# Column sums four abreast, float32r gate sums, two products of ones and a moved split in a TensorE-bound hybrid backbone

## The chip, the cores and the metric

The kernel runs on one core of one Trainium2 chip. A core has a matrix engine (TensorE, "PE" in the profile, with its weight loads "PEld"), VectorE ("DVE"), ScalarE ("ACT"), GpSimd ("POOL") and SyncE ("SP"), each with its own instruction queue. Here SP issues nearly all loads from the chip's main memory (HBM) and POOL the stores. TensorE multiplies a stationary tile (loaded as weights, here up to 128x128) with a moving tile of up to 512 columns and writes to PSUM, the accumulator memory; everything else reads and writes SBUF. The metric is the device time of one execution in microseconds (us).

## The reference

Two layers over 512 latent tokens and 256 context tokens, width 1024, all in float32. Layer 0 is bidirectional retention with 4 heads, layer 1 a chunked gMLP with a spatial gate. Around each layer stand a conditioned RMSNorm and a conditioned gate:

```python
silu_c = jax.nn.silu(c)
silu_cc = jax.nn.silu(c_ctx)
for i in range(DEPTH):                                   # DEPTH = 2
    shift_x, scale_x, gate_x = jnp.split(silu_c @ ada_w[i] + ada_b[i], 3, axis=-1)
    shift_c, scale_c, gate_c = jnp.split(silu_cc @ ada_w[i] + ada_b[i], 3, axis=-1)
    hx = rmsnorm(x, norm_g[i]) * (1 + scale_x[:, None]) + shift_x[:, None]
    hc = rmsnorm(ctx, norm_g[i]) * (1 + scale_c) + shift_c
    # i = 0: retention of hx and hc;  i = 1: gMLP of hx
    x = x + gate_x[:, None] * out_x
return rmsnorm(x, final_g)
```

Retention projects to q, k (256 per head), v and z (512 per head), turns q and k of the latent tokens by their grid position, weights the scores by a decay in both directions, normalizes the head's output, multiplies it with silu(z) and projects back to 1024. The gMLP projects to u, v and z of 2048 each, normalizes v, mixes it inside chunks of 128 tokens, and projects u * mixed * silu(z) back to 1024.

The change touches how four vectors of 1024 are made that are not needed at once: `gate_x` of layer 0, and shift, scale and gate of layer 1, each a product of `silu(c)` with a 1024x1024 block of `ada_w`.

## The kernel before

**Precision.** Each float32 operand of a large product is split in two float32r tiles, a high part (an ACT copy that rounds) and a low part (a DVE subtraction, `split`), and a product is three float32r products (`mm3`). In the trace the split tiles are called `hl`, the raw weights `raw`; `oA11` to `oA22` and `oS1` to `oS4` are split activations and their sums, `hc` the split context.

**Projections.** Layer 0's q, k, v and z are computed in twelve "quads" (`QUADS`). A "kq" quad makes k and q of one head with the weights stationary (`features`, shown as moving tile oA, oS or hc, stationary hl: `pst<-oA,hl`); a "vz" quad makes half of v and z of one head with the activations stationary (`tokens`, shown as `pst<-hl,oA`). A quad is a block product by seven products of sums (names B11, T1, T2, B21, T3, B22, T4); each is a group of 24 matmuls of 128x128 by 128x256, and B11 and B21 have a second group of 24 for the context. The first three quads are treated apart; the other nine are the loop over `QUADS[3:]`, numbered n = 0 to 8: vz, vz, kq, vz, vz, kq, vz, kq, vz. The quads n = 2, 5 and 7 are the second, third and fourth kq quad.

**Order.** PE runs in the order of the text. ACT and DVE are ordered by a scheduler at build time. Work that is not urgent is written as generators, and the loop takes single steps of them between products (`aside`, `step`): `background` makes the four vectors; `dec0`, `qk0` and `v0` prepare the decay, q and k, and v of head 0. `load_qk` issues five loads in three steps (k, q, k, the context's k, q), then splits each of the five tiles (`halves`) in a step of its own. `Q` streams the weights through slots w0 to w6 and splits them two products ahead.

**Background.** For each of the four vectors DVE multiplies 8 blocks of 128x1024 by a per-row scalar and adds them up in `a` (`ada_a` in the trace). What is left is a sum over the 128 rows. For the first three vectors `columns` does it: two f32 products with 32 columns of ones, each over 512 columns and each in its own 32 columns of the array; a copy of 64 rows to SBUF (`cole`); four transposes of 64x128 blocks; a DVE copy that picks out one column per block. For the fourth, two f32 products with 128x128 ones give the sum on all rows, and DVE adds a bias (`gateb1`). Three of these events lie among the projection quads, the fourth in the scores of head 2.

**Products of ones.** `between_modes` is one f32 product of a 128x128 tile of ones with itself whose result nobody reads. `inside_t` is a list of functions to be called inside the next `tokens` product, in front of its second of four blocks (behind 6 of its 24 matmuls). Before the change one is put there at n = 0.

After the projections come per head `attend` (scores, products with v, normalization) and `project_out`, then layer 1. Head 0's first scores read q and k as split by `load_qk`. Layer 1's first weights are read into freed slots, w2 and w3 among them, as soon as these come free.

Of the kernel before, what the change touches and what calls it, by code (L numbers as in the profile page):

```python
# [8 lines left out]
F32R = mybir.dt.float32r  # L9
# [4 lines left out]
P = 128  # L14
D = 1024
# [11 lines left out]
HS = 256  # L27
# [6 lines left out]
def f32(ap):  # L34
    return ap.bitcast(F32)
# [32 lines left out]
def hybrid_kernel(ctx, tc, xT_d, cT_d, cv_d, sv_d, rows_d, ada0_d, adag_d, w_d, rope_d, dec_d, ws_d, id_d, out_d):  # L68
    nc = tc.nc
    pe, act, dve, sp = (Queue(tc, e) for e in (nc.tensor, nc.scalar, nc.vector, nc.sync))  # L70
# [11 lines left out]
    def st(shape, tag, dt=F32, bufs=1, name=None):  # L82
        return sb.tile(shape, dt, tag=tag, name=name or tag, bufs=bufs)
# [34 lines left out]
    def t2(name, shape=(P, 512), dt=F32):  # L118
        return st(list(shape), "t2", dt, bufs=T2, name=name)

    def pt(shape=(P, 512), tag="ps"):
        return ps.tile(list(shape), F32, tag=tag, name="pst", bufs=6 if tag == "ps" else 2)

    mm = pe.matmul
# [7 lines left out]
    def split(hl, src, late=None):  # L132
        h, l = hl
        act.copy(h, src)
        low = lambda: dve.tensor_tensor(l, src, f32(h), ALU.subtract)
        if late is None:
            low()
        else:
            late.append(low)
# [4 lines left out]
    def load(dst, src):  # L144
        sp.dma_start(dst, src)
# [282 lines left out]
    ones = st([P, P], "ones")  # L428
# [3 lines left out]
    ident = st([P, P], "ident")  # L432
# [203 lines left out]
    def project(q):  # L636
        if q[0] == "kq":
            return Product(features, kq_done(q[1]), hc)
        return Product(tokens, vz_done(q[1], q[2]), hc)
# [192 lines left out]
    def ada_piece(i, tag, tags):  # L832
        a = st([P, D], tag, name="ada_a")
        rows = []
        for k in range(KT + 1):
            if k < KT:
                rows.append(bg_raw(tags))
                load(rows[k], adag_d[8 * i + k])
            if k == 0:
                yield None  # L840
                continue
            r, c = rows[k - 1], cpad[:, k - 1, 0:1]
            if k == 1:
                dve.tensor_scalar(a, r, c, None, ALU.mult)
            else:
                dve.scalar_tensor_tensor(a, r, c, a, ALU.mult, ALU.add)
            yield None
        yield a

    def columns(a, dst):  # L850
        pr = pt(tag="tm")
        for j in range(2):
            mm(pr[32 * j:32 * j + 32, :], ones[:, 0:32], a[:, j * 512:j * 512 + 512], start=True, stop=True)
        e = t2("cole")
        act.copy(e[0:64, :], pr[0:64, :])
        yield
        pq = pt((P, 4, 64), tag="tm")
        for b in range(4):
            pe.transpose(pq[:, b, :], e[0:64, b * P:b * P + P], ident[0:64, 0:64])
        v = pq.rearrange("p b (j r) -> p r j b", r=32)  # L860
        dve.tensor_copy(dst.rearrange("p (j b) -> p j b", j=2), v[:, 0, :, :])

    gate0 = st([P, KT], "gate0")
    gs1 = st([P, KT], "gs1")
# [3 lines left out]
    def background():  # L868
        for i in range(4):
            a = None  # L870
            for a in ada_piece(i, *(("g1", ("g2", "g3")) if i < 3 else ("oA22", ("w2", "w3")))):
                if a is None:
                    yield
            yield
            if i == 0:
                yield from columns(a, gate0)
                dve.tensor_tensor(gate0, gate0, gateb0, ALU.add)
            elif i == 1:
                yield from columns(a, sh1)
                dve.tensor_tensor(sh1, sh1, adab1[:, 0, :], ALU.add)  # L880
                dve.tensor_tensor(shs, sh1[:, 0:4], sh1[:, 4:8], ALU.add)
            elif i == 2:
                yield from columns(a, gs1)
                dve.tensor_tensor(gs1, gs1, adab1[:, 1, :], ALU.add)
                dve.scalar_tensor_tensor(gs1, gs1, 1.0, g1, ALU.add, ALU.mult)
            else:
                gb = st([P, D], "g1", name="gateb1")
                load(gb, rows_d[0:1, :].partition_broadcast(P))
                yield
                yield  # L890
                yield
                for j in range(2):
                    pr = pt(tag="tm")
                    mm(pr, ones, a[:, j * 512:j * 512 + 512], start=True, stop=True)
                    dve.tensor_tensor(gb[:, j * 512:j * 512 + 512], pr, gb[:, j * 512:j * 512 + 512], ALU.add)
                Q.gate = gb
            yield i

    bg = background()

    def aside(work):

        act.pinned = dve.pinned = True
        r = next(work, None)
        act.pinned = dve.pinned = False
        return r

    def step():
        return aside(bg)
# [83 lines left out]
    def popped():  # L993
        if later:
            later.pop(0)()
# [18 lines left out]
    v0 = load_v(0)  # L1014
    for n, q in enumerate(QUADS[3:]):
        pr = project(q)
        if n == 0:
            inside_t.append(between_modes)
        for i, name in enumerate(SINGLE):
            pr.run(name, Q.get())  # L1020
            if i % 2:
                popped()
            if 2 not in pieces and i not in (2, 4):
                pieces.append(step())
            if n == 5 and i % 2 == 0:
                aside(dec0)
            if n >= 6:
                aside(qk0)
            if n == 8:
                aside(v0)  # L1030
# [586 lines left out]
```

## Time and profile before

| | us |
|---|---|
| median of 3 runs (878.61 to 880.75) | 878.79 |
| profiled execution | 878.75 |
| its span, first to last instruction | 876.7 |
| PE busy in it | 866.0 |
| DVE busy | 712.2 |
| ACT busy | 457.2 |
| POOL busy | 58.3 |

Around the span lie 2.05 us. Rows of the profile name the engine, the operation, `out<-in` by the names of tiles (for a matmul: PSUM tile, moving tile, stationary tile), the shape and a count. In the timeline a row is a run of like instructions, with its start and its duration from the start of the first to the modelled end of the last; starts of neighbouring rows are the sounder measure. An f32 product that isn't a transpose leaves two records, a float32r product and a transpose one. All instructions have line L54, the helper that records them, so work is told apart by tile names.

### The profile page before, as it was taken

The page shows a single profiled execution, that of the slowest core. Times are in us where ns is not written, and L with a number is a line of the kernel's source. Part 1 is how long each engine was busy: PE and PEld are TensorE (multiplying, and loading weights), DVE is VectorE, ACT ScalarE, POOL GpSimd, SP SyncE. Part 2 cuts the span into 40 slices and gives each one's busy share as a digit, 9 for nine tenths or more (in the row PEclk, how much of TensorE's full clock was granted, in tenths as well). Part 3 has the DMA queues.
Part 4 walks back from the last instruction along what each step waited for, and adds up shares of the span by engine and source line. Part 5 has one row for each costly group of instructions (what it writes and reads, how often), then busy time and mean ns, then how long its engine had stood idle before and what let it go on. Part 6 is the DMA issues. An engine that isn't in the chain of part 4 may idle for free.

```text
span 876.7 us, 16965 instructions
## 1 busy us (share of the span) xinstructions
PE 866.0 (99%) x6890; PEld 826.8 (94%) x6890; DVE 712.2 (81%) x997; ACT 457.2 (52%) x707; POOL 58.3 (7%) x96
## 2 busy tenths in 40 slices
PE   8999999999999999999999999999999999999997
PEld 7799999999999999998989999999999899899986
DVE  4689978699789877878677688999899488688995
ACT  4465744444545435736255548844666546256434
POOL 0001211002101101000000001111000000000110
PEclk9999999999999999999999999999999999999999
DMA  9932967457677458848344511645435135035522
GB/s 349 405 129 97 303 239 267 150 174 241 193 237 243 145 165 328 286 127 272 132 156 158 165 52 70 200 153 196 142 133 180 36 121 192 25 121 168 121 44 102
DMA packets 75774, 153.81 MB, mean 175 GB/s; under 512 B 7728, under 2 KB 34864, under 8 KB 75696
## 3 DMA queue, kind: packets, MB, share of 16 engines
q1 hardware_dynamic: 67392, 128.40, 44.2%
q0 software_dynamic: 7872, 24.12, 8.2%
q8 instruction: 54, 0.88, 0.4%
q10 hardware_dynamic: 432, 0.20, 0.1%
q14 instruction: 24, 0.20, 0.1%
HBM read 128.58 MB, written 24.12 MB: 174 GB/s over the span
## 4 chain that ended last, share of the span: by engine, by line
PE 96%; DVE 1%; DMA 1%; ACT 1%; issue 0%; DVEq 0%; ACTq 0%
PE pst L54 96%; DMA raw<-in_w_dram 1%; DMA xq<-in_xT_dram 0%; DVE o L54 0%; ACT junk L54 0%; DVE xq L54 0%; DVE bnx L54 0%; DVE oA L54 0%; ACT oA L54 0%; ACT fss L54 0%; DVE gs L54 0%; DVE hl L54 0%; DVE sq L54 0%; ACT o L54 0%; DVE ada_s L54 0%
## 5 line engine op out<-in xcount | busy, mean ns | idle before, releaser
L54 DVE TENSOR_TENSOR hl<-raw,hl 128x1024 fp32r<-128x1024 f32 (+2 forms) x197 | 234.8, 1198 | 67.8 <-ACT hl L54 67.5
L54 ACT CAST hl<-raw 128x1024 fp32r<-128x1024 f32 (+2 forms) x197 | 202.8, 1033 | 137.1 <-DVE raw L54 59.3
L54 PE MATMUL pst<-oS,hl 128*128 128x256 f32 x1104 | 133.9, 279 | 0.1
L54 PE MATMUL pst<-hl,oS 128*128 128x256 f32 x1152 | 133.4, 276 | 0.0
L54 PEld LDWEIGHTS pst<-hl,oS 128*128 128x128 f32 x1152 | 131.8, 188 | 1.0 <-ACT snap L54 0.8
L54 PEld LDWEIGHTS pst<-oS,hl 128*128 128x128 f32 x1104 | 129.3, 188 | 1.6 <-PE pst L54 0.8
L54 PE MATMUL pst<-oA,hl 128*128 128x256 f32 x936 | 117.2, 280 | 1.7 <-DVE hl L54 1.2
L54 PEld LDWEIGHTS pst<-oA,hl 128*128 128x128 f32 x936 | 111.2, 188 | 4.5 <-DVE hl L54 1.6
L54 DVE TENSOR_TENSOR raw<-raw 128x1024 f32<-128x1024 f32 x92 | 111.9, 1218 | 0.8
L54 ACT COPY snap<-pst 128x512 f32<-128x512 f32 x92 | 53.6, 584 | 90.5 <-PE pst L54 90.3
L54 PE MATMUL pst<-hl,oA 128*128 128x256 f32 x768 | 91.6, 277 | 0.0
L54 PE MATMUL pst<-og,hl 128*128 128x256 f32 x768 | 91.1, 278 | 0.0
L54 PEld LDWEIGHTS pst<-og,hl 128*128 128x128 f32 x768 | 89.2, 188 | 0.3
L54 PEld LDWEIGHTS pst<-hl,oA 128*128 128x128 f32 x768 | 89.2, 188 | 0.1
L54 PE MATMUL pst<-v,ph 128*128 128x512 f32 x192 | 59.8, 393 | 0.0
L54 PE MATMUL pst<-hl,ya 128*128 128x512 f32 (+1 forms) x246 | 59.1, 386 | 0.0
L54 PEld LDWEIGHTS pst<-hl,ya 128*128 128x128 f32 x246 | 45.3, 188 | 9.5
L54 DVE TENSOR_TENSOR snap<-pst,snap 128x512 f32<-128x512 f32 x69 | 47.2, 684 | 6.2 <-PE pst L54 6.2
L54 PE MATMUL pst<-hl,hc 128*128 128x256 f32 x384 | 46.1, 276 | 0.0
L54 PEld LDWEIGHTS pst<-hl,hc 128*128 128x128 f32 x384 | 44.7, 188 | 0.0
L54 ACT CAST ph<-pf 128x512 fp32r<-128x512 f32 x24 | 14.8, 619 | 54.1 <-DVE pf L54 53.6
L54 PEld LDWEIGHTS pst<-v,ph 128*128 128x128 f32 x192 | 36.1, 188 | 7.3 <-issue 0.2
(181 smaller groups left out, 1022.3 us busy)
## 6 DMA issues: line engine op xcount, KB each, us to landing
raw<-in_w_dram SPq DMA_DIRECT2D x224, 256.0 KB, 4.1
bg<-in_adag_dram SPq DMA_DIRECT2D x32, 512.0 KB, 4.4
ada_w<-in_ada_dram SPq DMA_DIRECT2D x16, 512.0 KB, 9.1
raw<-in_w_dram SPq DMA_DIRECT2D x16, 512.0 KB, 4.3
bg<-in_dec_dram SPq DMA_DIRECT2D x12, 512.0 KB, 4.8
v<-snap POOLq DMA_DIRECT2D x16, 256.0 KB, 5.3
z<-snap POOLq DMA_DIRECT2D x16, 256.0 KB, 5.1
v<-v SPq DMA_DIRECT2D x8, 512.0 KB, 3.8
```

Of the source, the lines that this page charges most:

```text
L54: made = op(*args, **kw)
```

## The change

In `columns`, the two f32 products of 512 columns become four of 256, each in its own 32 columns of the array, so that the sum stands on 128 rows of 256; ACT copies 128x256 instead of 64x512; two transposes of 128x128 take the place of four of 64x128. For the fourth vector, `a` is split in a float32r pair in slots w2 and w3 (one ACT copy and one DVE subtraction of 128x1024), the ones are copied to float32r, and four float32r products that accumulate in pairs take the place of two f32 products. A product of ones is also put into the first token product of n = 3 and n = 8. And the steps of `qk0` are taken at the first three products of n = 6 and at all products of n = 8, where they were taken at every product from n = 6 on.

```diff
     def columns(a, dst):
-        pr = pt(tag="tm")
-        for j in range(2):
-            mm(pr[32 * j:32 * j + 32, :], ones[:, 0:32], a[:, j * 512:j * 512 + 512], start=True, stop=True)
-        e = t2("cole")
-        act.copy(e[0:64, :], pr[0:64, :])
+        pr = pt((P, HS), tag="tm")
+        for j in range(4):
+            mm(pr[32 * j:32 * j + 32, :], ones[:, 0:32], a[:, j * HS:j * HS + HS], start=True, stop=True)
+        e = t2("cole", (P, HS))
+        act.copy(e, pr)
         yield
-        pq = pt((P, 4, 64), tag="tm")
-        for b in range(4):
-            pe.transpose(pq[:, b, :], e[0:64, b * P:b * P + P], ident[0:64, 0:64])
+        pq = pt((P, 2, P), tag="tm")
+        for b in range(2):
+            pe.transpose(pq[:, b, :], e[:, b * P:b * P + P], ident)
...
                 load(gb, rows_d[0:1, :].partition_broadcast(P))
+                ones_r = st([P, P], "rs0", F32R, name="ones_r")
+                act.copy(ones_r, ones)
+                hl = [st([P, D], tag, F32R, name="ada_h") for tag in ("w2", "w3")]
                 yield
+                split(hl, a)
                 yield
                 yield
                 for j in range(2):
                     pr = pt(tag="tm")
-                    mm(pr, ones, a[:, j * 512:j * 512 + 512], start=True, stop=True)
+                    for m in range(2):
+                        mm(pr, ones_r, hl[m][:, j * 512:j * 512 + 512], start=m == 0, stop=m == 1, skip_group_check=True)
...
         pr = project(q)
-        if n == 0:
+        if n in (0, 3, 8):
             inside_t.append(between_modes)
...
-            if n >= 6:
+            if n == 8 or (n == 6 and i < 3):
                 aside(qk0)
```

How the instructions stand, at the places that matter. The first is PE in the second kq quad (n = 2), where the first background piece is summed: rows are products in their order, moving tile before stationary tile, with the number of the buffer behind some names.

```order
 L54 MATMUL pst<-oA_291,hl 128x256 x24
 L54 MATMUL pst<-hc,hl 128x256 x24
-L54 MATMUL pst<-ada_a,ones 32x512 x2
+L54 MATMUL pst<-ada_a,ones 32x256 x4
 L54 MATMUL pst<-oS_865,hl 128x256 x24
-L54 MATMUL pst<-ident,cole 128x64 x4
+L54 MATMUL pst<-ident,cole 128x128 x2
 L54 MATMUL pst<-oS_1013,hl 128x256 x24
 L54 MATMUL pst<-oA_574,hl 128x256 x24
```

Sums and transposes keep their places; their shapes and counts change. The second piece stands the same way in a vz quad, the third in the fourth kq quad (n = 7).

The second is PE at the end of that kq quad and the start of the vz quad behind it (n = 3); the same difference stands behind the fourth kq quad (n = 8).

```order
 L54 MATMUL pst<-oS_1177,hl 128x256 x24
 L54 MATMUL pst<-oA_576,hl 128x256 x24
-L54 MATMUL pst<-hl,oA_291 128x256 x24
+L54 MATMUL pst<-hl,oA_291 128x256 x6
+L54 MATMUL pst<-ones 128x128
+L54 MATMUL pst<-hl,oA_291 128x256 x18
 L54 MATMUL pst<-hl,hc 128x256 x24
 L54 MATMUL pst<-hl,oS_865 128x256 x24
```

The product of ones goes behind the sixth matmul of the first token product.

The third is the gate sum. On PE, among the products of head 2's weights with v:

```order
 L54 MATMUL pst<-v,pl 128x512
 L54 MATMUL pst<-v,ph 128x512 x2
-L54 MATMUL pst<-ada_a,ones 128x512 x2
+L54 MATMUL pst<-ada_h,ones_r 128x512 x4
 L54 MATMUL pst<-v,pl 128x512
 L54 MATMUL pst<-v,ph 128x512 x2
```

The place is the same, the products are others. On DVE, at the end of head 1's output projection (accumulator updates, then the first score weights of head 2):

```order
-L54 SCALAR_TENSOR_TENSOR acc<-pst,gate_896,acc 128x256 x8
+L54 SCALAR_TENSOR_TENSOR acc<-pst,gate_896,acc 128x256 x5
+L54 TENSOR_TENSOR ada_h<-ada_a,ada_h 128x1024
+L54 SCALAR_TENSOR_TENSOR acc<-pst,gate_896,acc 128x256 x4
 L54 SCALAR_TENSOR_TENSOR pf<-pst,dt 128x512
 L54 TENSOR_TENSOR pl<-pf,ph 128x512
```

The low part of the split comes between the accumulator updates (the piece of the difference also moved one update from in front of v's splits).

The fourth is ACT in the last quad (n = 8), up to the split of v. Before:

```order
L54 COPY snap<-pst 128x512
L54 CAST hl<-raw 128x1024
L54 COPY snap<-pst 128x512
L54 CAST hl<-raw 128x1024
L54 COPY snap<-pst 128x512
L54 ACTIVATE snap<-snap 128x512
L54 CAST v<-v 128x1024
```

And after:

```order
L54 CAST qk<-qk 128x512
L54 CAST hl<-raw 128x1024
L54 COPY snap<-pst 128x512
L54 CAST qk<-qk 128x512
L54 CAST hl<-raw 128x1024
L54 COPY snap<-pst 128x512
L54 CAST qk<-qk 128x512
L54 CAST hl<-raw 128x1024
L54 COPY snap<-pst 128x512
L54 CAST qk<-qk 128x512
L54 ACTIVATE snap<-snap 128x512
L54 CAST qk<-qk 128x512
```

The five copies of q and k, which stood among the splits of the seventh and eighth quad, stand between those of the last; the subtractions on DVE follow them in the same way.

More of the change, by code (lines that the diff above doesn't have):

```diff
@@ L850, in columns @@
     def columns(a, dst):
-        pr = pt(tag="tm")
-        for j in range(2):
-            mm(pr[32 * j:32 * j + 32, :], ones[:, 0:32], a[:, j * 512:j * 512 + 512], start=True, stop=True)
-        e = t2("cole")
-        act.copy(e[0:64, :], pr[0:64, :])
+        pr = pt((P, HS), tag="tm")
[3 more added lines that the diff above has]
+        act.copy(e, pr)
         yield
-        pq = pt((P, 4, 64), tag="tm")
-        for b in range(4):
-            pe.transpose(pq[:, b, :], e[0:64, b * P:b * P + P], ident[0:64, 0:64])
+        pq = pt((P, 2, P), tag="tm")
+        for b in range(2):
+            pe.transpose(pq[:, b, :], e[:, b * P:b * P + P], ident)
         v = pq.rearrange("p b (j r) -> p r j b", r=32)
-        dve.tensor_copy(dst.rearrange("p (j b) -> p j b", j=2), v[:, 0, :, :])
+        dve.tensor_copy(dst.rearrange("p (j b) -> p j b", j=4), v[:, 0, :, :])
     gate0 = st([P, KT], "gate0")
```

## The prediction

> **What bounds the kernel now.** I read the page first: its times, the busy table and the chain that ended last.
>
> ```profile
> span 876.7 us, 16965 instructions
> PE 866.0 (99%) x6890; PEld 826.8 (94%) x6890; DVE 712.2 (81%) x997; ACT 457.2 (52%) x707; POOL 58.3 (7%) x96
> PE 96%; DVE 1%; DMA 1%; ACT 1%; issue 0%; DVEq 0%; ACTq 0%
> ```
>
> PE is busy for 99% of the span and is 96% of the chain. The view of waits, for PE, starts with its largest entry:
>
> ```profile
> PE pst L54 <- DVE sq L54: 1.4, 2, 1.2
> ```
>
> The largest total that PE waited for anybody is 1.4 us. So this kernel's time is the sum of what PE issues, one instruction behind the other, and an edit counts if it takes something out of that row, puts something in, or changes the pace of what stays. Moving work between ACT and DVE counts only if PE ends up waiting. A busy PE says nothing of its pace, though; that is read from start times in the timeline. Columns there: start, duration of the merged row, operation, count. I use differences of starts, since the ends of pipelined matmuls are modelled.
>
> The change touches four places on PE. The second background piece (a column sum, then transposes) lies in a run of token products:
>
> ```profile
> 222.44 2.88 PE L54 MATMUL pst<-hl,hc 128*128 128x256 f32 x24
> 225.25 1.05 PE L54 MATMUL pst<-ada_a,ones 128*32 128x512 f32 x4
> 226.23 5.73 PE L54 MATMUL pst<-hl,oS 128*128 128x256 f32 x48
> 231.89 0.46 PE L54 MATMUL pst<-ident,cole 64*128 64x64 f32 x4
> 232.28 3.01 PE L54 MATMUL pst<-hl,oA 128*128 128x256 f32 x24
> 235.12 2.99 PE L54 MATMUL pst<-oA,hl 128*128 128x256 f32 x24
> ```
>
> The sums hold PE from 225.25 to 226.23, 0.98 us, and the transposes from 231.89 to 232.28, 0.39 us. (An ordinary f32 product shows as two records, a transpose as one.) A product of ones, as the change adds two, stands here, with an undisturbed group behind it:
>
> ```profile
> 108.70 0.38 PE L54 MATMUL pst<-ones 128*128 128x128 f32 x2
> 108.84 2.30 PE L54 MATMUL pst<-hl,oA 128*128 128x256 f32 x18
> 110.98 2.88 PE L54 MATMUL pst<-hl,hc 128*128 128x256 f32 x24
> 113.70 0.28 PE L54 MATMUL pst<-hl,oS 128*128 128x256 f32 x1
> ```
>
> The undisturbed group takes 113.70 - 110.98 = 2.72 us for 24, 113 ns each: the fast pace. A features product (weights stationary) runs at another one:
>
> ```profile
> 292.37 5.92 PE L54 MATMUL pst<-oS,hl 128*128 128x256 f32 x48
> 298.13 2.99 PE L54 MATMUL pst<-oA,hl 128*128 128x256 f32 x24
> 300.96 2.99 PE L54 MATMUL pst<-hc,hl 128*128 128x256 f32 x24
> 312.26 2.90 PE L54 MATMUL pst<-hl,oA 128*128 128x256 f32 x24
> 315.00 1.18 PE L54 MATMUL pst<-hl,hc 128*128 128x256 f32 x9
> ```
>
> Here 24 take 300.96 - 298.13 = 2.83 us, 118 ns each, although the shape is the same. This pace is not fixed to the kind of product, as the start of the program shows below, so it is a term of its own.
>
> **The change part by part: the column sums.** Three pieces. Two f32 products of 512 columns become four of 256, each in its own 32 columns of the array. The same form stands in the conditioning of layer 0:
>
> ```profile
> 21.45 1.07 PE L54 MATMUL pst<-ada_w,cpad 128*32 128x256 f32 x16
> 22.45 0.97 PE L54 MATMUL pst<-oA,hl 128*128 128x256 f32 x6
> ...
> 24.89 0.84 PE L54 MATMUL pst<-oS,hl 128*128 128x256 f32 x6
> 25.66 1.93 PE L54 MATMUL pst<-ada_w,cpad 128*32 128x256 f32 x32
> 27.52 1.68 PE L54 MATMUL pst<-oA,hl 128*128 128x256 f32 x12
> ```
>
> Sixteen records (8 products) take 22.45 - 21.45 = 1.00 us and 32 take 27.52 - 25.66 = 1.86, so 16 more cost 0.86 and 8 more 0.43. The change's 8 records then take 1.00 - 0.43 = 0.57 us in place of 0.98. Gain 0.41 each, 1.23 for three. Ends: 0 (the four do not run abreast) and 0.98 - 0.43 = 0.55 each (no fixed part); I take 0.41, since it comes from the same form. The Trainium skill, page "TensorEngine Tiling (Array Packing)", section Theoretical Speedup, gives up to 2x for 64 columns and 4x for 32. Read so, going from two abreast to four would halve the 0.98 and gain an estimated 0.49 each, 0.24 us more in all; the rows have a fixed part that the rule leaves out, and I go by the rows.
>
> **The transposes.** Four of 64 rows become two of the full 128, which the conditioning also has:
>
> ```profile
> 49.39 1.52 PE L54 MATMUL pst<-oA,hl 128*128 128x256 f32 x12
> 50.75 0.38 PE L54 MATMUL pst<-ident,adae 128*128 128x128 f32 x2
> 50.89 1.66 PE L54 MATMUL pst<-oA,hl 128*128 128x256 f32 x12
> 52.38 1.58 PE L54 MATMUL pst<-hc,hl 128*128 128x256 f32 x12
> 53.80 1.46 PE L54 MATMUL pst<-oA,hl 128*128 128x256 f32 x11
> ```
>
> They take 50.89 - 50.75 = 0.14 us in place of 0.39. The 12 products ahead of them take 1.36 us, 113 ns each, while the 24 ahead of the sums in the piece above take 2.81, 0.09 over 2.72: a change of tile shape holds PE up before it starts. The new transposes have the shape of their neighbours, so I count that 0.09 too: 0.34 each, 1.02 for three (ends 0.75 without it and 1.1 with the start-up behind them).
>
> **The gate sums.** Two f32 products become four float32r ones amid the score-value products:
>
> ```profile
> 452.59 0.39 PE L54 MATMUL pst<-v,pl 128*128 128x512 f32 x1
> 452.82 0.63 PE L54 MATMUL pst<-v,ph 128*128 128x512 f32 x2
> 453.29 1.88 PE L54 MATMUL pst<-ada_a,ones 128*128 128x512 f32 x4
> 454.60 0.80 PE L54 MATMUL pst<-v,pl 128*128 128x512 f32 x1
> 455.24 0.63 PE L54 MATMUL pst<-v,ph 128*128 128x512 f32 x2
> ```
>
> Three float32r products of 512 take 453.29 - 452.59 = 0.70, 0.23 each. The f32 sums and the held-up product behind them take 455.24 - 453.29 = 1.95, less 0.23 is 1.72. Four float32r products take 0.92. Gain 0.80 (0.4 if the product behind is still held up). Added for it: one ACT copy and one DVE subtraction of 128x1024 and a small copy of ones. By the order of the instructions the subtraction falls into head 1's output projection, four accumulator updates ahead of head 2's first scores, and its reader stands behind all but the last of that head's scores. The new tiles take slots w2 and w3, so two pairs of weight loads wait on the SP queue for the gate sums, and head 3's v loads and one load of head 2's output weights stand behind them; those v loads wait for PE's score-value products of the same place anyway. Their first reader among the next layer's splits cannot be earlier than this:
>
> ```profile
> L54 ACT CAST hl_e<-raw x4: 1043/1048/1053, 492.8 to 523.0; 128x1024 fp32r<-128x1024 f32 x4
> ```
>
> 492.8 is 38 us behind the sums. Cost nothing; if that cover were gone, the layer's first split would wait for one load.
>
> **The two products of ones** cost 108.84 - 108.70 = 0.14 us each, and the 18 behind them take 2.14 in place of 18 x 0.1133 = 2.04. So 0.24 each, 0.48 lost. Token products reach the fast pace without one (below), so I see no gain in the same quad.
>
> **The moved splits** of head 0's q and k are five pairs:
>
> ```profile
> L54 ACT CAST qk<-qk x20: 604/618/633, 277.6 to 462.5; 128x512 fp32r<-128x512 f32 x20
> L54 DVE TENSOR_TENSOR qk<-qk x20: 677/681/687, 279.8 to 464.2; 128x512 fp32r<-128x512 f32 x20
> 312.00:337.00 25.00, 25.00 (x223) 25.00 (x222) 16.18 (x23) 10.16 (x13) 4.04 (x7) 1.00 0.74 255
> ```
>
> That adds 5 x 0.68 = 3.4 us to DVE's 16.2 in the last quad's 25 us, and 3.1 to ACT's 10.2 (columns of the last row: window, sum, PE, PEld, DVE, ACT, POOL). Both keep over 5 us free. The loads stay where they were in the seventh quad. Cost nothing; at worst the halves come late for head 0's scores at the end of this window, bounded by all five subtractions behind it: 3.4 us.
>
> **The pace.** In front of the transposes at 50.75 the features products ran at 113 ns; behind them 12 take 53.80 - 52.38 = 1.42 us, 118 ns: slow. At 24.89, behind two transposes and six more products, six take 0.77 us, and less the 0.09 ahead of the next form that is 113 ns: fast. So a disturbance within features products can leave either pace, and it lasts. The rest of the second kq quad behind its transposes is 6 groups of 24, that of the fourth is 7 (292.37 to 312.26); both are slow before. Each group that turns fast gains 2.83 - 2.72 = 0.11: 0.66 and 0.77 us. They have nothing to lose, as they are slow already; only the 20 or so products between sums and transposes of the first piece, partly fast now, could lose 0.1. I take one of the two as turning fast, the middle of the span 0 to 1.43. The Trainium skill says in "TensorE: Matmul & The Clock Gate", Part 2, step 1, that loading the next weights does not steal read bandwidth from the running matmul. By that rule the two kinds of product would have one pace, nothing would turn, and the sum would end without this term, as in rival 1; the rows at 298.13 and 110.98 disagree, and I go by them.
>
> **Sum.** -1.23 - 1.02 - 0.80 + 0.48 = -2.57, and -0.7 for one stretch: -3.3. The profiled execution took 878.75 us, of which 876.7 are the span; the median of the runs is 878.79, the same within 0.04. Forecast 875.5.
>
> **Rivals.**
> 1. The sum alone, pace unchanged: 878.75 - 2.57 = 876.2. For it: the slow stretch behind 50.75, which has the very transposes that are put in. Against it: the rows at 24.89.
> 2. The four sums do not overlap, or the transposes still hold PE up: the change does not do what it says. Without the 1.23 it is 877.4, without the 1.02 as well 878.4. Against it: 0.43 per 8 records in the conditioning, the same form.
> 3. Slower: the token quads lose their fast pace. They show one slow case, in the next layer:
>
> ```profile
> 536.27 3.04 PE L54 MATMUL pst<-hl_e,oA 128*128 128x256 f32 x24
> 539.15 1.04 PE L54 MATMUL pst<-ident,acc 128*128 128x128 f32 x8
> ```
>
> 24 in 2.88 us, 0.16 over the fast group. If the features quads end in the other state and the four token quads behind them (nine groups each) ran so, it would be 36 x 0.16 = 5.8 us: 876.2 + 5.8 = 882.0. It decides from 16 groups on (2.57 / 0.16), two whole quads. For it: entry decides the pace elsewhere. Against it: at 312.26 tokens follow features and 24 take 315.00 - 312.26 = 2.74 us, and a product of ones now stands in two of the four.
>
> **How the numbers follow.** About 0.3% (2.6 us) is what a measurement of this kernel can tell from no change; the bound is 876.15. Both stretches fast, 874.8: 0.25. One fast, 875.4: 0.31. Sum alone, 876.2: 0.26, on the bound, so 0.07 of it counted as faster. Rival 2: 0.08. Slower than before by the pace or by late halves, the latter at most 876.2 + 3.4 = 879.6: 0.10, of which 0.07 by over 0.3%. Faster 0.63, within 0.3% 0.30, slower 0.07. The range runs from both stretches fast less 0.4 for the upper ends of the terms, 874.4, to rival 2's lower end and a little, 877.6; it leaves out the slower cases and most of rival 2.
>
> **What would show it.** Right: column sums at 0.57 us, transposes at 0.14 with no delay ahead, the gate sums at 0.92, ones at 0.24, and the groups behind the transposes of the second or fourth kq quad at 2.72 per 24. Wrong: PE waits on qk or ph near the first scores; token groups at 2.8 or more; sums at 0.98; a new wait on raw in the next layer.

## The result and the profile after

| | before | after |
|---|---|---|
| median of runs, us | 878.77 (878.29 to 880.75, 6 runs) | 875.32 (875.12 to 875.86, 6 runs) |
| profiled execution, us | 878.75 | 875.4 |
| its span, us | 876.7 | 873.3 |
| PE busy in it, us | 866.0 | 862.7 |

The ratio is 0.9957, 95% interval 0.9947 to 0.9967. The forecast was 875.5. The head of the page after:

```profile
span 873.3 us, 16994 instructions
PE 862.7 (99%) x6900; PEld 826.2 (95%) x6900; DVE 714.2 (82%) x998; ACT 458.5 (52%) x709; POOL 58.4 (7%) x96
PE 96%; DVE 1%; DMA 1%; ACT 1%; issue 0%; DVEq 0%; ACTq 0%
```

PE is the same 96% of the chain, and its busy time fell by 3.3 us where the span fell by 3.4. The view of waits for PE has no wait on the halves of q and k, on the gate's split or on the next layer's weights. All its entries lie in the first 60 us, ahead of the places of the change; the largest is this one:

```profile
PE pst L54 <- DVE sq L54: 1.2, 1, 1.2
```

So the gain lies in PE's own row. The timeline of PE (start, duration, operation, count; I use differences of starts) at the first piece, the second kq quad:

```profile
162.90 0.64 PE L54 MATMUL pst<-ada_a,ones 128*32 128x256 f32 x8
163.47 0.38 PE L54 MATMUL pst<-oS,hl 128*128 128x256 f32 x1
...
166.32 0.38 PE L54 MATMUL pst<-ident,cole 128*128 128x128 f32 x2
166.46 2.98 PE L54 MATMUL pst<-oS,hl 128*128 128x256 f32 x24
169.28 2.88 PE L54 MATMUL pst<-oA,hl 128*128 128x256 f32 x24
172.00 0.28 PE L54 MATMUL pst<-hc,hl 128*128 128x256 f32 x1
```

The sums take 163.47 - 162.90 = 0.57 us and the transposes 0.14. Behind them a features group takes 172.00 - 169.28 = 2.72 us for 24, the fast pace. Before, the same group took 173.03 - 170.20 = 2.83:

```profile
167.27 3.09 PE L54 MATMUL pst<-oS,hl 128*128 128x256 f32 x24
170.20 2.99 PE L54 MATMUL pst<-oA,hl 128*128 128x256 f32 x24
173.03 2.99 PE L54 MATMUL pst<-hc,hl 128*128 128x256 f32 x24
...
184.34 2.90 PE L54 MATMUL pst<-hl,oA 128*128 128x256 f32 x24
```

The same in the fourth kq quad, where the group that took 2.83 before takes 2.72 (from the row at 295.26 to the next group at 297.98):

```profile
289.71 5.70 PE L54 MATMUL pst<-oS,hl 128*128 128x256 f32 x48
295.26 2.88 PE L54 MATMUL pst<-oA,hl 128*128 128x256 f32 x24
...
308.86 0.88 PE L54 MATMUL pst<-hl,oA 128*128 128x256 f32 x6
```

The token quad behind the second kq quad, with its product of ones:

```profile
182.88 0.88 PE L54 MATMUL pst<-hl,oA 128*128 128x256 f32 x6
183.59 0.38 PE L54 MATMUL pst<-ones 128*128 128x128 f32 x2
183.73 2.30 PE L54 MATMUL pst<-hl,oA 128*128 128x256 f32 x18
185.86 1.41 PE L54 MATMUL pst<-hl,hc 128*128 128x256 f32 x11
```

The six matmuls ahead of the ones take 0.71 us, 118 ns each: this quad was entered at the slow pace, which it was not before. The gate sums take 451.03 - 450.12 = 0.91 us, and the product behind them starts on time:

```profile
449.65 0.63 PE L54 MATMUL pst<-v,ph 128*128 128x512 f32 x2
450.12 1.08 PE L54 MATMUL pst<-ada_h,ones_r 128*128 128x512 f32 x4
451.03 0.39 PE L54 MATMUL pst<-v,pl 128*128 128x512 f32 x1
```

One place that the change does not touch got slower, the first v stage of layer 1. Before:

```profile
549.18 22.24 PE L54 MATMUL pst<-hl,oS 128*128 128x256 f32 x192
571.26 0.84 PE L54 MATMUL pst<-hl,oA 128*128 128x256 f32 x6
```

And after:

```profile
545.19 22.88 PE L54 MATMUL pst<-hl,oS 128*128 128x256 f32 x192
567.90 0.87 PE L54 MATMUL pst<-hl,oA 128*128 128x256 f32 x6
```

The same 192 matmuls take 571.26 - 549.18 = 22.08 us before and 567.90 - 545.19 = 22.71 after, 0.63 more. By terms:

| term | forecast, us | measured, us |
|---|---|---|
| column sums, three | -1.23 | -1.2 (0.57 each) |
| transposes, three | -1.02 | -1.02 |
| gate sums | -0.80 | -0.81 |
| two products of ones | +0.48 | +0.49 (24 with the ones 2.98, the same 24 before 2.74) |
| pace behind the transposes | -0.7 | -1.39 (-0.65 and -0.74) |
| layer 1's first v stage | 0 | +0.63 |
| sum | -3.3 | -3.3, of 3.4 in the span |

The pace is read from the end of the transposes to the first token product: 184.34 - 167.27 = 17.07 us before and 182.88 - 166.46 = 16.42 after in the second kq quad, 312.26 - 292.37 = 19.89 and 308.86 - 289.71 = 19.15 in the fourth.

### The profile page after: what moved, and what is told of

Its sections match the earlier page's. It is cut to its first block, busy times and chain, and to the rows that moved or that the text cites. A ratio compares the mean times of both kernels' runs of the same rounds, so it can differ in the third digit from the quotient of the medians.

```text
span 873.3 us, 16994 instructions
## 1 busy us (share of the span) xinstructions
PE 862.7 (99%) x6900; PEld 826.2 (95%) x6900; DVE 714.2 (82%) x998; ACT 458.5 (52%) x709; POOL 58.4 (7%) x96
## 4 chain that ended last, share of the span: by engine, by line
PE 96%; DVE 1%; DMA 1%; ACT 1%; issue 0%; DVEq 0%; ACTq 0%
PE pst L54 96%; DMA raw<-in_w_dram 1%; DMA xq<-in_xT_dram 0%; DVE o L54 0%; ACT junk L54 0%; DVE xq L54 0%; DVE bnx L54 0%; DVE oA L54 0%; ACT oA L54 0%; ACT fss L54 0%; DVE gs L54 0%; DVE hl L54 0%; DVE sq L54 0%; ACT o L54 0%; DVE ada_s L54 0%
```

## The experiments

Each kernel is compared with runs of the kernel before on the same chip (878.6 to 879.0 us in all of them).

**1. Without the two products of ones.**

```diff
-        if n in (0, 3, 8):
+        if n == 0:
             inside_t.append(between_modes)
```

> The changed kernel without the two added products of ones. Theory: a pace, once entered, lasts until PE is disturbed; the features quads now end fast, and token products entered from there start slow (the six ahead of each product of ones took 0.71 us, 118 ns each). Without the ones the nine groups of the first vz quad and six of the next, up to the second column sum, run at 118 ns, and the nine groups of the last quad too: 24 x 0.11 = +2.6 us, less 0.48 for the products left out: 877.4 us. Rival, as the prediction had it: token products reach the fast pace by themselves within four matmuls, so leaving the ones out gains 0.48: 874.8 us.

Measured: 876.88 us (876.22 to 878.30, 11 runs), ratio 0.9979 (0.9971 to 0.9988): 1.56 us slower than with the products. The profiled execution is the longest of these, 878.3 us. PE's timeline behind the second kq quad:

```profile
186.23 2.99 PE L54 MATMUL pst<-hl,hc 128*128 128x256 f32 x24
189.06 1.22 PE L54 MATMUL pst<-hl,oS 128*128 128x256 f32 x9
```

189.06 - 186.23 = 2.83: the token products stay slow, and do so up to the next column sum, and again in the last quad. In this changed kernel the two products buy far more than they cost. The theory's 877.4 us lies within the interval.

**2. Only the two products of ones, in the kernel before.**

```diff
-        if n == 0:
+        if n in (0, 3, 8):
             inside_t.append(between_modes)
```

> The kernel before with the two products of ones alone. Theory: there the features quads end slow and the token products behind them recover by themselves, so the two products only cost 2 x 0.24: 879.25 us, and every group of the features quads keeps 2.83 us. Rival: the products of ones are what makes the quads fast wherever they stand: then the time falls below 878.77.

Measured: 879.24 us (878.77 to 879.71, 11 runs), ratio 1.0007 (0.9998 to 1.0015), and in the profile the 24 products with the ones among them take 0.24 us more than the 2.74 of the kernel before. The expectation that every group of the features quads stays slow did not hold in this execution: the second kq quad is fast.

```profile
169.80 2.88 PE L54 MATMUL pst<-oA,hl 128*128 128x256 f32 x24
172.52 2.88 PE L54 MATMUL pst<-hc,hl 128*128 128x256 f32 x24
```

172.52 - 169.80 = 2.72. Up to this place the program is that of the kernel before, old transposes included, which was slow here in its profile. So this place has taken either pace behind the old transposes, and the cause of that is open. Behind it the tokens are entered slow (184.11 - 183.40 = 0.71 us for six) and the product of ones turns them fast; behind the fourth kq quad, which is slow here, the tokens recover by themselves and the product only costs. So the value of this edit depends on the pace of the quad ahead.

**3. The gate sums in float32 again.**

```diff
-                    for m in range(2):
-                        mm(pr, ones_r, hl[m][:, j * 512:j * 512 + 512], start=m == 0, stop=m == 1, skip_group_check=True)
+                    mm(pr, ones, a[:, j * 512:j * 512 + 512], start=True, stop=True)
```

(and the split and its tiles left out)

> The changed kernel with the gate sums back in f32 and without their split. By the sum of PE's row: +0.80 us, 876.1 us, with the v product behind the sums held up again. Rival: the gain of 3.4 us was made elsewhere and the sums are hidden: 875.3 us. The stretch of layer 1 that turned slow may turn back, which would take 0.65 from either.

Measured: 875.74 us (875.33 to 876.31, 5 runs), 0.42 more than the changed kernel, half of the term. In the profiled execution, 875.33 us:

```profile
449.83 1.88 PE L54 MATMUL pst<-ada_a,ones 128*128 128x512 f32 x4
...
451.79 0.39 PE L54 MATMUL pst<-v,ph 128*128 128x512 f32 x1
...
545.73 22.24 PE L54 MATMUL pst<-hl,oS 128*128 128x256 f32 x192
567.81 0.84 PE L54 MATMUL pst<-hl,oA 128*128 128x256 f32 x6
```

The sums and the product held up behind them take 451.79 - 449.83 = 1.96 again, where the four sums and that product take 0.91 + 0.23 in the changed kernel: +0.82. But layer 1's first v stage is at 22.08 us in this execution. The term is as forecast, and here a stretch 95 us later hides most of it; whether it does so in the other four runs is not shown.

**4. Head 0's q and k split from the seventh quad on, as before.**

```diff
-            if n == 8 or (n == 6 and i < 3):
+            if n >= 6:
                 aside(qk0)
```

> The changed kernel with the splits of head 0's q and k back in the seventh and eighth quad. Theory: PE waits for neither place, so the time stays at 875.3 us within 0.2 us, or a stretch turns its pace and it moves by some 0.6 us. Rival: the move is worth something, since DVE is busy for 25.7 of the 26 us from 261 on in the kernel before: then PE shows waits for hl there and the time is above 876 us.

Measured: 876.20 us (875.65 to 878.61, 6 runs), 0.88 more than the changed kernel. PE's timeline in the fourth kq quad, in the profiled execution (878.61 us, which also lost 1.8 us in its first 10 us):

```profile
295.53 3.09 PE L54 MATMUL pst<-oS,hl 128*128 128x256 f32 x24 [0.84 <-DVE hl L54]
298.46 1.81 PE L54 MATMUL pst<-oA,hl 128*128 128x256 f32 x14
```

PE waits 0.84 us for the low part of a split, and the rest of the fourth kq quad behind this wait is slow. On DVE, which has no gap from 283 to 295 us, subtractions of q and k stand among the splits (one of the three between 284 and 292 us is shown):

```profile
291.38 0.69 DVE L54 TENSOR_TENSOR qk<-qk 128x512 fp32r<-128x512 f32 x1
291.99 1.22 DVE L54 TENSOR_TENSOR raw<-raw 128x1024 f32<-128x1024 f32 x1
293.12 2.35 DVE L54 TENSOR_TENSOR hl<-raw,hl 128x1024 fp32r<-128x1024 f32 x2
```

PE waits for the second split of the last row, which ends at 295.47. In the kernel before, with q and k at the same place, DVE does the same work within 0.1 us of these times:

```profile
293.03 1.22 DVE L54 TENSOR_TENSOR hl<-raw,hl 128x1024 fp32r<-128x1024 f32 x1
294.17 0.16 DVE L54 COPY gs<-pst 128x8 f32<-128x8 f32 x1
294.24 1.21 DVE L54 TENSOR_TENSOR hl<-raw,hl 128x1024 fp32r<-128x1024 f32 x1
```

There PE starts the same product at 295.30 without a wait, though the second split ends only at 295.45. The order of the two built programs explains it: the two splits stand the other way round. In the kernel before, the one that PE needs next (of the product T2) is the first and that of T3, which PE reaches 8 us later, the second; in the kernel of this experiment T3's is the first. PE was ready at 295.53 - 0.84 = 294.69, only 0.6 us earlier than in the kernel before; with T2's split in the first place, done at about 294.3, it would not have waited in this execution. So the wait comes from the order that the scheduler gave these two splits; the time that the other edits save ahead of it does not make it by itself. In the changed kernel T2's split is ahead of T3's. Why the scheduler turned them round is not shown. Whether the move gains anything by itself was not run; PE in the kernel before has no wait at this place that it could take away.

**5. Column sums and transposes as before.**

```diff
-        for j in range(4):
-            mm(pr[32 * j:32 * j + 32, :], ones[:, 0:32], a[:, j * HS:j * HS + HS], start=True, stop=True)
+        for j in range(2):
+            mm(pr[32 * j:32 * j + 32, :], ones[:, 0:32], a[:, j * 512:j * 512 + 512], start=True, stop=True)
...
-        for b in range(2):
-            pe.transpose(pq[:, b, :], e[:, b * P:b * P + P], ident)
+        for b in range(4):
+            pe.transpose(pq[:, b, :], e[0:64, b * P:b * P + P], ident[0:64, 0:64])
```

> The changed kernel with the column sums and the transposes as in the kernel before (two abreast, four 64 by 64 transposes). Whether the features stretches turned fast by this part of the change, or by something else in it. Theory: this part gives 3 x 0.41 + 3 x 0.34 = 2.25 directly, and its transposes turn the second and the fourth k and q quad fast (0.62 + 0.75): +3.6 against the changed kernel's 875.32, less up to 0.65 where layer 1's first v stage turns fast again: 878.3 to 878.9 us. Rival: the pace of these quads comes from elsewhere (the two products of ones, the moved splits): 877.6 us, or 876.9 with layer 1 fast.

Measured: 878.40 us (877.86 to 879.17, 11 runs), ratio 0.9997 (0.9988 to 1.0006). The second kq quad is slow again:

```profile
170.46 2.99 PE L54 MATMUL pst<-oA,hl 128*128 128x256 f32 x24
173.29 0.99 PE L54 MATMUL pst<-hc,hl 128*128 128x256 f32 x7
```

173.29 - 170.46 = 2.83. So is the fourth (2.82 for its group at 298.63). With its direct gain this part of the change is nearly the whole of the result, 3.1 of 3.4 us. The fourth kq quad is slow behind the old transposes in all three profiles that have them and fast behind the new ones in all ten, apart from the wait of experiment 4, so its pace belongs to this part. The second is fast behind the new ones in all ten too, but behind the old ones it was slow twice and fast once (experiment 2), so how much of its 0.65 us the change brings on the average is open.

**6. The products of ones at n = 3 and n = 8 in float32r.**

```diff
-            inside_t.append(between_modes)
+            inside_t.append(between_modes if n == 0 else between_r)
```

(`between_r` is the same product of a float32r copy of the ones)

> The changed kernel, but the products of ones at n = 3 and n = 8 are taken in float32r, as the features and token products around them are, not in float32. Whether any interruption of the row brings the fast pace back behind the features, or only one with a float32 product. Theory A (the change of type and the restart behind it do it): the token products at these two places stay at 118 ns, as in the kernel without the two products, and the end is near that kernel's 876.9 us: 876.3 to 877.3. Theory B (any product of another shape between them does it): 113 ns behind the products, which are then shorter than the 0.24 us of the float32 ones: 875.0 to 875.4 us.

Measured: 874.89 us (874.45 to 875.47, 5 runs), ratio 0.9957 (0.9944 to 0.9969).

```profile
183.70 0.22 PE L54 MATMUL pst<-ones_r 128*128 128x128 f32 x1
183.76 2.27 PE L54 MATMUL pst<-hl,oA 128*128 128x256 f32 x18
185.87 1.30 PE L54 MATMUL pst<-hl,hc 128*128 128x256 f32 x10
```

The product takes 0.06 us in place of 0.14, the 18 behind it 2.11 in place of 2.13, and the groups that follow run at 2.72. The median lies a little below theory B's range, and theory A falls: the type is not what brings the fast pace back.

**7 to 9. More products of ones:** one in layer 1's first v stage (7), one in the third kq quad and one in the token quad behind it (8), and all three (9).

```diff
+        if n == 5:
+            inside.append(between_modes)
-        if n in (0, 3, 8):
+        if n in (0, 3, 6, 8):
...
+                if (a, name, q) == (0, "T1", 0):
+                    inside_t.append(between_modes)
```

> The changed kernel, with one more float32 product of ones inside the first part of layer 1's first v stage, where the profile of the changed kernel showed 192 products at 117.8 ns (545.19 to 567.90 us) that the kernel before had run at 113 to 115 ns. Theory: the product costs 0.24 us and turns the rest of these products fast, which gives back 0.65 us: 874.9 us, 874.5 to 875.2. Rival: the slow stretch is a matter of the single execution and as often fast as not, so that the product buys half of that or less: 875.2 to 875.5 us. Second rival: the pace there is not set by the entry, and the product only costs: 875.56 us.

> The changed kernel, with one more float32 product of ones inside the third k and q quad (n = 5), whose features run at 2.83 us per 24 in both profiles (233.21 to 258.65 us), and one inside the token quad behind it (n = 6), since the two runs of the products of ones showed that token quads behind fast features enter slow. Theory: the features turn fast, 9 groups by 0.11 = -0.97, two products at +0.24: -0.49, so 874.8 us, 874.4 to 875.1. Rival: the features stay slow behind a product of ones, as they did not behind the new transposes: +0.48, 875.8 us.

> The changed kernel with the three further products of ones of the two kernels ahead together. Theory: their gains add, -0.41 and -0.49: 874.4 us, 874.0 to 874.9. Rival: each stretch that is made fast moves the entry of a later one, which can turn slow, as layer 1's first v stage did with this change: 874.9 to 875.6 us.

Measured: 875.11 (874.64 to 876.95), 874.47 (874.39 to 874.94) and 874.30 us (874.14 to 874.85), five runs each; ratios 0.9962 (0.9949 to 0.9974), 0.9952 (0.9938 to 0.9965) and 0.9951 (0.9939 to 0.9964). Of the third kq quad, kernel 8:

```profile
235.86 0.38 PE L54 MATMUL pst<-ones 128*128 128x128 f32 x2
...
236.78 2.88 PE L54 MATMUL pst<-hc,hl 128*128 128x256 f32 x24
239.50 2.77 PE L54 MATMUL pst<-oS,hl 128*128 128x256 f32 x23
```

239.50 - 236.78 = 2.72: a features quad turns fast behind such a product as well. In layer 1 the product gains 0.21 by the medians (875.32 to 875.11), half of the 0.41, and 0.17 on top of kernel 8, differences that the intervals do not tell from nothing. They fit the rival: in the nine profiles without it the stage took 22.08 to 22.09 us in five and 22.71 to 22.72 in four, so the product has something to win in some executions and not in others. Each kernel has one profile, so whether the pace goes by kernel or by execution stays open.

**10. The three further products, and all from the first kq quad on in float32r.**

```diff
+    ones_r = st([P, P], "rs0", F32R, name="ones_r")
+    act.copy(ones_r, ones)
+    square.append(ones_r)
     bg = background()
...
-        mm(pr, ones, ones, start=True, stop=True)
+        mm(pr, one, one, start=True, stop=True)
```

(`one` is the float32r copy once it has been written; it turned out that this took in one product more, at 59.6 us in the third quad, twelve in all and not eleven)

> The kernel with the three further products of ones, and all its products of ones from the first k and q quad on (eleven of them) in float32r. The two float32r products of the run with these alone moved the row by 0.09 and 0.10 us against the float32 ones and left the pace behind them fast. Theory: eleven times 0.09 to 0.10, -1.0 to -1.1 against that kernel's 874.30: 873.3 us, 873.0 to 873.8. Rival: in some of the nine other places the float32r product does not bring the fast pace back, as its gap behind is 169 ns and not 201; one token quad of 24 groups that stays slow costs 0.11 per group, so one such place takes all of the gain back: 874.0 to 876 us.

Measured: 878.72 us (876.60 to 882.04, 8 runs), ratio 1.0009 (0.9993 to 1.0025): neither the theory nor the rival. PE's timeline in the third quad, and the stretches behind (window, sum, PE, granted clock, DMA share, GB/s):

```profile
62.17 0.33 PE L54 MATMUL pst<-ones_r 128*128 128x128 f32 x1 [2.99 <-ACT ones_r L54]
62.33 3.17 PE L54 MATMUL pst<-hl,oA 128*128 128x256 f32 x18
65.30 3.64 PE L54 MATMUL pst<-hl,hc 128*128 128x256 f32 x24
68.77 0.39 PE L54 MATMUL pst<-hl,oA 128*128 128x256 f32 x2
```

```profile
62.00:64.00 2.00, 1.83 (x13) 0.87 0.26 109
64.00:66.00 2.00, 2.00 (x12) 0.50 0.07 25
66.00:68.00 2.00, 2.00 (x16) 0.78 0.74 260
```

The copy of the ones stood behind other work on ACT, and the first product waited 2.99 us for it. Behind the wait TensorE was granted half the clock for a while, and 42 matmuls (18 and 24) took 68.77 - 62.33 = 6.44 us, 1.6 more than the 4.86 of the kernel of experiment 9 by its own rows (2.14 and 2.72). So 3.0 us of waiting cost 4.6. The Trainium skill's page "TensorE: Matmul & The Clock Gate", Part 1, tells of such a halving after a free-running window of some 3.4 us without work; the trace agrees in kind, with a gap of 2.99 us being enough. Behind this place each float32r product moved the row by 0.10 to 0.13 us to the good, as the theory had it. The eight runs spread over 5.4 us, and this profile shows one of them.

**11. The first of these twelve back in float32.**

```diff
-    inside_t.append(between_modes)
+    inside_t.append(lambda: between_modes(ones))
```

> The kernel ahead with its first product of ones (at 59.6 us, where TensorE waited 2.99 us for ScalarE's float32r copy of the ones and was then granted half the clock for some 3 us) back in float32, so that the copy is an engine's work with 47 us to spare before the next product of ones takes it. Ten products stay float32r. Theory: no wait and no drop of the clock, and ten times 0.09 to 0.12 against the kernel with the three further products in float32, 874.30: 873.3 us, 873.0 to 873.7. Rival: ScalarE's copy of 0.30 us ahead of the splits delays these in any place, and the row waits for a split: 873.7 to 875.

Measured: 873.47 us (873.28 to 875.07, 5 runs), ratio 0.9944 (0.9930 to 0.9957). Eleven products are float32r here, not ten. The wait is gone, and PE's largest is again the one of 1.2 us for DVE. This is the fastest kernel of the study, 1.85 us below the changed one by the medians.

## Why the prediction was right, and where it was not

**Right: PE's row is the bound, and its direct terms.** The column sums (0.57), the transposes (0.14, nothing ahead of them), the gate sums (0.91) and the price of a product of ones (0.24) came out within 0.03 us of their rows each, because each had a row of the same form or shape elsewhere in the program. The Trainium skill's page "TensorEngine Tiling (Array Packing)", section Theoretical Speedup, would have halved the 0.98 to an estimated 0.49; the measured 0.57 is on the side of the rows. Experiments 3 and 5 undid these parts but the ones, and PE's row gave them back.

**Mis-sized: the pace behind the transposes.** The prediction took one of the two stretches as turning fast, -0.7, and gave both a chance of 0.25. Both turned: -1.39. For the fourth kq quad experiment 5 shows that this part of the change does it; the second has been fast once behind the old transposes as well (experiment 2). That the number still hits within 0.2 us is in part luck, since two errors cancel: 0.63 us were lost in layer 1's first v stage, for which the prediction had no term. That stage has two durations, 22.08 and 22.71, and nine profiles of kernels that are alike there fall on both; it is no effect that can be tied to one edit.

**Wrong: "Token products reach the fast pace without one, so I see no gain in the same quad".** This read the kernel before, where the features ahead of those quads are slow. Behind fast features the quads are entered slow and stay so without the products (experiment 1, 1.56 us). In the sum the step was right by its size, since the products restore the pace that the quads had; in its reason it was wrong, and rival 3, "the token quads lose their fast pace", was a real danger, though of 1.6 us and not of 5.8.

**Amended: the moved splits at nothing.** In the kernel before there is no wait at the old place that the move could take away. In the changed kernel the old place costs 0.88 us in the medians: PE waits 0.84 us for a split, because the one for a later product was put ahead of it (experiment 4). The prediction looked only at where the work goes, the last quad's spare DVE time, and not at what it leaves, a stretch in which DVE had no gap and the order of its splits decides whether PE waits.

**Not seen.** No wait on q and k, on the gate's split, or on layer 1's weights: the covers that the prediction named held.

## What to carry to other kernels

When one engine's row is the whole time, price each edit from a row of the same form, but then ask of every stretch behind it whether it will be entered as before: here it decided the pace of quads of 216 matmuls, and moved half as much time as the edits themselves. Where an engine beside the bound one has no gap left, look at the order in which the build puts its work: one piece in front of the piece that is needed next was worth 0.84 us of waiting. An edit that costs in the kernel before can pay in the kernel after, so a set of edits is tried with one left out, not only with one put in.

## What the runs showed that was not expected

**Two paces that last.** Float32r matmuls of 128x128 by 128x256, each with its own weights, run at 113 or at 118 ns in whole stretches, in features as in token products, and keep their pace until something else, or the other kind of product, comes. It is not the granted clock: from 170 to 182 us, within the second kq quad, this is 1.00 in the profile before, slow there, and in the profile after, fast there. The table gives the pace of the ninth to the 22nd matmul behind such an event, in the 13 profiled executions:

| behind | fast | slow |
|---|---|---|
| a product of ones, float32 or float32r | 124 | 0 |
| the new transposes at 166 us | 10 | 0 |
| the new transposes at 230 us | 0 | 10 |
| the new transposes at 290 us | 10 | 0 |
| the old transposes at 167 us | 1 | 2 |
| the old transposes at 232 us | 3 | 0 |
| the old transposes at 292 us | 0 | 3 |

(One product of ones is left out, that behind which the clock was halved.) The same place gives nearly always the same pace, but the same transposes give either at different places. One product of 128 columns among those of 256 has always brought the fast pace, for 0.24 us in float32 and 0.13 in float32r (0.06, and 2.11 - 2.04 behind it), and it is no matter of the type. The change from features to tokens has a regularity too, at the ends of the second, third and fourth kq quad in the 13 profiles: behind fast features the tokens came in slow in 24 of 24 cases, and stayed so until the product of ones or, without one, the next column sum or the end of the quads; behind slow features they went over to the fast pace by themselves in 15 of 15. That is why the products of ones pay behind the quads that the change turns fast, and only cost behind slow ones. What sets the pace inside the engine these traces do not show, and it stays open; so does why layer 1's first v stage falls on either side.

**A short wait costs more than itself.** 2.99 us of idle TensorE cost 4.6 us, by the granted clock of 0.50 behind it. PE's wait of 1.2 us for DVE at 43 us, in the profiles before and after, leaves the granted clock at 1.00.
